# Probabilities transposed by VectorE blocks and DMAs through DRAM for 21 of 24 heads, instead of by TensorE

## The chip, the cores and the metric

The kernel runs on one core of a Trainium2 chip. The metric is the device time of one execution in microseconds; three runs of the kernel before gave 2160.7, 2161.55 and 2162.31 us.

The core's engines work side by side, each through its own instruction stream in order, and wait for one another through semaphores: TensorE (matrix products; PE in the profile, its weight loads PEld), VectorE (DVE), ScalarE (ACT), GpSimd (POOL), and SyncE (SP), which here only issues DMAs. ScalarE and GpSimd can issue DMAs too; the profile shows such issues as ACTq and POOLq.

## The reference

Two decoder layers on 256 tokens of width 2048, all in float32. Layer 0 mixes tokens by attention with a forget gate (FoX, 16 heads of width 128), layer 1 by a mixture of three dilated windows (8 heads, three groups each, values of width 256). Each mixer and each MLP is preceded by a root-mean-square norm. What is around the change is the attention:

```python
def one_block(args):                      # FoX, one block of 128 queries
    i, q_i, c_i = args
    s = jnp.einsum('bqhd,bkhd->bhqk', q_i, k, preferred_element_type=jnp.float32) * scale
    s = s + jnp.transpose(c_i, (0, 2, 1))[..., None] - c_keys[:, :, None, :]
    s = jnp.where(causal, s, -jnp.inf)
    p = jax.nn.softmax(s, axis=-1)
    return jnp.einsum('bhqk,bkhd->bqhd', p.astype(v.dtype), v)
...
s = jnp.where(valid[None, None, :, None], s + alibi, -jnp.inf)     # dilated, one group
m = jnp.max(s, axis=-1)
p = jnp.exp(s - m[..., None])
...
num = jnp.sum(w[..., None] * jnp.stack(nums, 0), axis=0)           # three groups merged
o = (num / den[..., None]).reshape(B, S, H * dv).astype(h.dtype)
```

The product of probabilities and values sums over keys. TensorE sums over partitions, so it needs the probabilities with keys on partitions, while the scores come with queries on partitions: each head's probabilities have to be transposed, three blocks of 128x128 (queries 0 to 127 see one block of keys, queries 128 to 255 see two).

## The kernel before

**Products.** All large products are split so that a float32 factor becomes a high part in the faster fp32r format and a low part that is the rest; a product is then three matmuls (high x high, high x low, low x high). Weights are streamed: SyncE loads `raw` tiles of two 128-row chunks x 512 columns (line 287), ScalarE casts them to `wh` (line 308, the *cast*), VectorE subtracts to get `wl` (line 309, the *cut*). There are five buffers of each. `product_steps` consumes them: one *step* is one 128-row chunk, six matmuls (lines 339 to 341, two token blocks), and after every second step `split` issues the cast and the cut for the buffer pair that has just come free.

**Order of the side work.** The attention chains are Python generators in `Jobs`. After every step `jobs.tick()` resumes those that are due: `yield 4` means "four steps later", `yield key` means "when that key is done". So the order in which work stands in each engine's stream is written out by hand in steps of the product loop. `behind(x)` makes the instructions in its block follow instruction x on the same engine (`issued["cast"]`, `issued["cut"]` and `issued["product"]` are the latest of each).

**FoX.** j runs over four groups of four heads; each j has a query, a key and a value product of 16 steps. `qk_chain` normalizes queries and keys and already transposes them by VectorE's 32x32 blocks, four DMA writes to DRAM per token block (line 543, issued by SyncE) and one read back (line 544, by GpSimd). Then `fox_head` starts for each head hh at step `4 * hh + 2` (for j = 3 at `3 * hh + 2`) after the keys are done: scores on TensorE (lines 714 and 620 to 623), bias, mask and maximum on VectorE (722, 725), exponential on ScalarE (728), normalization on VectorE (733), then `p_transposed`, and three steps later `pv`.

**Dilated heads.** q4 runs over four groups of two heads; `dil_head` starts at step `6 * i + 2`, does scores of the three groups one step apart into the single tile `sd` (line 769), merges the groups into `p` (783 to 786), then `p_transposed`, and two steps later `pv`, twice (two halves of the value's width).

**`p_transposed`** (line 591 on) makes three TensorE transposes into a PSUM bank of the tag `tp` (line 594), then three copies out of it: `p_hi` by ScalarE (598), `p_lo` by VectorE (599), `p_whole` by ScalarE (600). The first two blocks of columns (keys 0 to 127 for both query blocks) are split in high and low; the third stays float32. **`pv`** multiplies them with the values (lines 586 and 587) and copies the result out (588, 589). Work tiles of the tag `s` (scores, probabilities, small constants) share four buffers.

The output projections follow: `out_proj` with `pair=True` runs 12 of 16 chunks for each of the first two column blocks (24 steps), then the last four chunks of each, so that the heads that come last are needed last.

## Time and profile before

| what | value |
|---|---|
| median of three runs | 2161.55 us (2160.7 to 2162.31) |
| the profiled execution's own time | 2161.91 us |
| its span, first to last instruction | 2160.2 us |
| transposes of line 594, FoX heads | 48, in 16 triples |
| transposes of line 594, dilated heads | 24, in 8 triples |
| ScalarE's `p_hi` / `p_whole` copies (lines 598, 600), FoX | 372 ns / 264 ns |
| VectorE's `p_lo` subtraction (line 599) | 417 ns |
| VectorE's block transpose of 128x512 (line 436) | 691 ns |
| bytes moved by all DMAs | 459.34 MB |

In the profile a line such as "182.05 0.49 PE L594 MATMUL ptp_f<-ident,s_f 128*128 128x128 f32 x3" says: at 182.05 us from the start of the span, for 0.49 us, TensorE executed three matmuls of source line 594 that wrote the tile `ptp_f`. Matmuls overlap one another, so what one costs is the distance to the next start, not its own duration. "[1.54 <-PE acc L341]" behind a line is the time for which the engine was idle before it, and what it waited for. A DMA row gives its issuing queue, the size of one, and the median time from issue to landing.

### The profile page before, as it was taken

To read this page: it belongs to the slowest core of one execution; us is meant where nothing else is said; L and a number is where in the kernel's file an instruction comes from. 1 tells how busy PE (TensorE), PEld (TensorE's weight loads), DVE (VectorE), ACT (ScalarE), POOL (GpSimd) and SP (SyncE) were. 2 spreads that over 40 slices of the span, in tenths; PEclk is the share of its full clock that TensorE was granted. 3 is DMA by queue.
4 is the path that set the end of the run, shared out by engine and by line. 5 is a ranking of instruction groups with operands and counts; after the bars stand their busy time and mean duration, and the time that the engine had idled before them with its cause. 6 is when DMAs were issued, how large, how long until landed. Compare 5 with 4: busy or idle time off the path is not lost.

```text
span 2160.2 us, 30057 instructions
## 1 busy us (share of the span) xinstructions
PE 2147.8 (99%) x11208; PEld 1912.6 (89%) x11208; DVE 1397.9 (65%) x1862; ACT 1105.9 (51%) x1545; POOL 74.1 (3%) x92
## 2 busy tenths in 40 slices
PE   9999999999999999999999999999999999999999
PEld 7888888988998998998888888888988988988988
DVE  6777787765655565566668777676655655655664
ACT  6565655644544454455555565546544543544442
POOL 1111000000000000000011010100000000000000
PEclk9999999999999999999999999999999999999999
DMA  7676667766666666667776776758666666666664
GB/s 251 220 225 196 224 201 233 248 203 204 199 203 205 200 201 204 203 199 241 244 242 207 232 226 195 259 177 275 215 204 201 200 204 204 198 203 204 202 210 144
DMA packets 292354, 459.34 MB, mean 213 GB/s; under 512 B 21944, under 2 KB 104432, under 8 KB 292208
## 3 DMA queue, kind: packets, MB, share of 16 engines
q1 hardware_dynamic: 288416, 446.27, 66.1%
q0 software_dynamic: 3232, 10.50, 1.4%
q8 instruction: 87, 1.43, 0.3%
q10 hardware_dynamic: 560, 0.66, 0.1%
q14 instruction: 59, 0.48, 0.1%
HBM read 438.48 MB, written 18.87 MB: 212 GB/s over the span
## 4 chain that ended last, share of the span: by engine, by line
PE 92%; DVE 3%; DMA 2%; issue 1%; ACT 1%; POOL 0%; SPq 0%; DVEq 0%; ACTq 0%; POOLq 0%
PE acc L340 19%; PE acc L341 19%; PE acc L339 19%; PE up_n1a_acc L403 5%; PE up_n3a_acc L403 5%; PE up_n3a_sc L403 3%; PE up_n1a_tp L403 3%; PE up_n1a_sc L403 3%; PE up_n3a_tp L403 3%; PE up_n3a_acc L407 3%; PE up_n1a_acc L407 3%; DMA raw<-in_dil_w_in_dram 2%; DVE wl L309 1%; PE up_n3a_tp L407 1%; PE up_n1a_sc L407 1%; PE up_n1a_tp L407 1%
## 5 line engine op out<-in xcount | busy, mean ns | idle before, releaser
L309 DVE TENSOR_TENSOR wl<-raw,wh 128x1024 fp32r<-128x1024 f32 (+1 forms) x801 | 975.0, 1221 | 686.7 <-ACT wh L308 681.0
L308 ACT CAST wh<-raw 128x1024 fp32r<-128x1024 f32 (+1 forms) x801 | 837.7, 1048 | 931.7 <-PE acc L341 567.4
L339 PE MATMUL acc<-wh,hT_n 128*128 128x512 f32 x896 | 343.0, 384 | 0.5 <-ACT wh L308 0.5
L340 PE MATMUL acc<-wl,hT_n 128*128 128x512 f32 x896 | 339.9, 379 | 0.1
L341 PE MATMUL acc<-wh,hT_n 128*128 128x512 f32 x896 | 339.5, 379 | 0.0
L339 PE MATMUL acc<-wh,aTh_n1a 128*128 128x512 f32 x512 | 194.0, 379 | 0.0
L340 PE MATMUL acc<-wl,aTh_n1a 128*128 128x512 f32 x512 | 194.0, 379 | 0.0
L341 PE MATMUL acc<-wh,aTl_n1a 128*128 128x512 f32 x512 | 194.0, 379 | 0.0
L341 PEld LDWEIGHTS acc<-wh,hT_n 128*128 128x128 f32 x896 | 169.3, 189 | 24.1
L339 PEld LDWEIGHTS acc<-wh,hT_n 128*128 128x128 f32 x896 | 169.6, 189 | 23.4 <-ACT wh L308 0.9
L340 PEld LDWEIGHTS acc<-wl,hT_n 128*128 128x128 f32 x896 | 169.8, 190 | 22.6 <-DVE wl L309 0.4
L339 PE MATMUL acc<-wh,aTh_n3a 128*128 128x512 f32 x480 | 181.9, 379 | 0.0
L340 PE MATMUL acc<-wl,aTh_n3a 128*128 128x512 f32 x480 | 181.9, 379 | 0.0
L341 PE MATMUL acc<-wh,aTl_n3a 128*128 128x512 f32 x480 | 181.9, 379 | 0.0
L403 PE MATMUL up_n1a_acc<-hT_n,wh 128*128 128x512 f32 x512 | 181.6, 382 | 0.0
L403 PE MATMUL up_n3a_acc<-hT_n,wh 128*128 128x512 f32 x512 | 181.6, 382 | 0.0
L407 PE MATMUL up_n1a_acc<-hT_n,wl 128*128 128x256 f32 x512 | 139.6, 273 | 0.0
L407 PE MATMUL up_n3a_acc<-hT_n,wl 128*128 128x256 f32 x512 | 139.6, 273 | 0.0
L341 PEld LDWEIGHTS acc<-wh,aTl_n1a 128*128 128x128 f32 x512 | 96.8, 189 | 13.8
L340 PEld LDWEIGHTS acc<-wl,aTh_n1a 128*128 128x128 f32 x512 | 96.8, 189 | 13.7
L339 PEld LDWEIGHTS acc<-wh,aTh_n1a 128*128 128x128 f32 x512 | 96.8, 189 | 13.6
L403 PEld LDWEIGHTS up_n3a_acc<-hT_n,wh 128*128 128x128 f32 x512 | 96.8, 189 | 13.5
(725 smaller groups left out, 3202.3 us busy)
## 6 DMA issues: line engine op xcount, KB each, us to landing
raw<-in_mlp_w_up_dram SPq DMA_DIRECT2D x256, 512.0 KB, 4.1
raw<-in_mlp_w_down_dram SPq DMA_DIRECT2D x256, 512.0 KB, 4.2
raw<-in_dil_w_in_dram SPq DMA_DIRECT2D x192, 256.0 KB, 4.6
raw<-in_fox_w_in_dram SPq DMA_DIRECT2D x95, 512.0 KB, 4.1
raw<-in_fox_w_out_dram SPq DMA_DIRECT2D x32, 512.0 KB, 4.3
raw<-in_dil_w_in_dram SPq DMA_DIRECT2D x32, 512.0 KB, 4.4
raw<-in_dil_w_out_dram SPq DMA_DIRECT2D x32, 512.0 KB, 4.4
blocks_n<-turned_n SPq DMA_DIRECT2D x96, 64.0 KB, 2.4
```

Of the source, the lines that this page charges most:

```text
L308: issued["cast"] = nc.scalar.copy(hi[:, part, :], raw[:, part, :])
L309: issued["cut"] = nc.vector.tensor_sub(lo[:, part, :], raw[:, part, :], hi[:, part, :].bitcast(F32))
L339: nc.tensor.matmul(acc[t], ah[:, tok], hi, start=first, stop=False)
L340: nc.tensor.matmul(acc[t], ah[:, tok], lo, start=False, stop=False)
L341: issued["product"] = nc.tensor.matmul(acc[t], al[:, tok], hi, start=False, stop=last)
L403: issued["product"] = nc.tensor.matmul(banks[b], hi[:, i, col], in_turn(tokens.rearrange("p x s -> p (x s)"), P // 2), start=first, stop=last)
L407: nc.tensor.matmul(banks[b][:, 0:S], lo[:, i, col], in_turn(tokens[:, 0, :], P // 2), start=False, stop=False)
```

## The change

For all heads but the last two of FoX's j = 3 and the last dilated one, `p_transposed` gives way to two new functions. `p_turned` has VectorE transpose the probabilities in 32x32 blocks into a tile `turned` (tag `s`), writes it to DRAM by four DMAs one step later, and four steps after that reads it back by one DMA, in the order that makes it a full transpose; all five are issued on ScalarE's queue, behind the latest cast. Another four steps later `p_split` makes `p_hi` (ScalarE) and `p_lo` (VectorE, behind the latest cut) from it; the third block is used where it lies. `pv` follows two steps after the split. The split parts are now kept in the order of the tokens, `pv` reads them with the two token blocks interleaved and writes its PSUM tile so; `by_token` undoes this when the result is copied out. `pv`'s matmuls are put behind the latest product. The tag `s` has five buffers instead of four and also holds `p_whole`. The heads of j = 3 start at steps 0, 2, 4, 7 instead of 0, 3, 6, 9, and the second head of q4 = 3 starts 3 steps after the first instead of 6.

```diff
+S_BUFS = 5
...
+    def by_token(po):
+        return po[:, 0:S].rearrange("p (n b) -> p b n", b=2)
...
     def pv(pt_sb, vt, cols, o_hi, o_lo, name):
...
-            for v, p, first in ((v_hi, p_hi, True), (v_hi, p_lo, False), (v_lo, p_hi, False)):
-                nc.tensor.matmul(po[:, 0:S], v[:, c:c + P], in_turn(p, P), start=first, stop=False)
-            nc.tensor.matmul(po[:, P:S], whole[:, c:c + P], p_whole, start=False, stop=True)
-            nc.scalar.copy(o_hi[i], po[:, 0:S])
-            nc.vector.tensor_sub(o_lo[i], po[:, 0:S], o_hi[i].bitcast(F32))
+            with behind(issued["product"]):
+                for v, p, first in ((v_hi, p_hi, True), (v_hi, p_lo, False), (v_lo, p_hi, False)):
+                    nc.tensor.matmul(po[:, 0:S], v[:, c:c + P], p.rearrange("p (b n) -> p n b", b=2), start=first, stop=False)
+                nc.tensor.matmul(by_token(po)[:, 1], whole[:, c:c + P], p_whole, start=False, stop=True)
+            hi, lo = (o.rearrange("p (b n) -> p b n", b=2) for o in (o_hi[i], o_lo[i]))
+            nc.scalar.copy(hi, by_token(po))
+            nc.vector.tensor_sub(lo, by_token(po), hi.bitcast(F32))
+
+    def p_turned(p, name):
+        turned = work.tile([P, 4, 3, 32], F32, tag="s", name=f"turned_{name}", bufs=S_BUFS)
+        nc.vector.transpose(turned.rearrange("p j b r -> p b j r"), p.rearrange("p (b j c) -> p b j c", b=3, c=32))
+        yield 1
+        blocks = dram.tile([4, 32, 4, 3 * 32], F32, tag="pblocks", name=f"pblocks_{name}", bufs=4)
+        for i in range(4):
+            with behind(issued["cast"]):
+                nc.scalar.dma_start(blocks[:, :, i, :].rearrange("j c x -> c j x"),
+                                    turned[32 * i:32 * i + 32].rearrange("p j b r -> p j (b r)"))
+        yield 4
+        with behind(issued["cast"]):
+            nc.scalar.dma_start(turned.rearrange("p i b r -> p (i b r)"), blocks.rearrange("j c i x -> (j c) (i x)"))
+        yield 4
+        return turned
+
+    def p_split(turned, name):
+        p_hi, p_lo = (work.tile([P, S], F32R, tag=f"pT{x}", name=f"pT{x}_{name}", bufs=2) for x in "hl")
+        first = turned.rearrange("p i b r -> p b i r")[:, 0:2]
+        hi, lo = (x.rearrange("p (b i r) -> p b i r", b=2, i=4) for x in (p_hi, p_lo))
+        with behind(issued["cast"]):
+            nc.scalar.copy(hi, first)
+        with behind(issued["cut"]):
+            nc.vector.tensor_sub(lo, first, hi.bitcast(F32))
+        return p_hi, p_lo, turned[:, :, 2, :]
...
     def p_transposed(p, name):
...
-        p_whole = work.tile([P, P], F32, tag="pTw", name=f"pTw_{name}", bufs=2)
-        first = by_column(pt[:, 0:S], P)
-        nc.scalar.copy(halves(p_hi, P), first)
-        nc.vector.tensor_sub(halves(p_lo, P), first, halves(p_hi, P).bitcast(F32))
+        p_whole = work.tile([P, P], F32, tag="s", name=f"pTw_{name}", bufs=S_BUFS)
+        nc.scalar.copy(p_hi, pt[:, 0:S])
+        nc.vector.tensor_sub(p_lo, pt[:, 0:S], p_hi.bitcast(F32))
...
     def fox_head(j, hh, qT, kT, vt, sel):
...
-        yield (3 if j == 3 else 4) * hh + 2
+        yield ((0, 2, 4, 7) if j == 3 else (0, 4, 8, 12))[hh] + 2
...
-        yield 2
-        pt_sb = p_transposed(block(s), f"f{h}")
-        yield ("fv", j)
-        yield 3
+        if j == 3 and hh > 1:
+            yield 2
+            pt_sb = p_transposed(s, f"f{h}")
+            yield 1
+        else:
+            turned = yield from p_turned(s, f"f{h}")
+            yield ("fv", j)
+            pt_sb = p_split(turned, f"f{h}")
+        yield 2
...
     def dil_head(q4, i, qTs, kTs, vt):
...
-        yield 6 * i + 2
+        yield (3 if q4 == 3 else 6) * i + 2
...
-        yield 2
-        pt_sb = p_transposed(block(p), f"d{h}")
-        yield ("dv", q4)
+        if (q4, i) == (3, 1):
+            yield 2
+            pt_sb = p_transposed(p, f"d{h}")
+        else:
+            turned = yield from p_turned(p, f"d{h}")
+            yield ("dv", q4)
+            pt_sb = p_split(turned, f"d{h}")
         yield 2
```

## The prediction

> **What bounds the kernel now.** I read the page first: its busy shares, the chain that ended last, then the waits, the windows and the timelines of single heads.
>
> ```profile
> span 2160.2 us, 30057 instructions
> PE 2147.8 (99%) x11208; PEld 1912.6 (89%) x11208; DVE 1397.9 (65%) x1862; ACT 1105.9 (51%) x1545; POOL 74.1 (3%) x92
> ...
> PE 92%; DVE 3%; DMA 2%; issue 1%; ACT 1%; POOL 0%; SPq 0%; DVEq 0%; ACTq 0%; POOLq 0%
> ```
>
> TensorE leaves 12.4 us idle in 2160.2, and 92% of the ending chain is its own work. So time taken from TensorE is time gained, if nothing that it then waits for is later than before. VectorE and ScalarE have room on average, but not everywhere: the windows show the fox heads of j=1, those of j=3, and the dilated heads of q4=2.
>
> ```profile
> 154.00:190.00 36.00, 36.00 (x194) 32.09 (x193) 29.00 (x60) 22.13 (x47) 1.66 (x1) 1.00 0.61 173
> 292.00:325.00 33.00, 33.00 (x181) 29.65 (x180) 29.34 (x68) 19.19 (x42) 0.53 (x2) 1.00 0.51 168
> 1310.00:1345.00 35.00, 35.00 (x191) 31.32 (x190) 28.58 (x49) 21.16 (x37) 1.66 (x1) 1.00 0.59 189
> ```
>
> Columns after the stretch are PE, PEld, DVE, ACT, POOL busy, granted clock, DMA share. VectorE is busy 81%, 89% and 82% there, ScalarE 61%, 58% and 60%.
>
> **What is removed from TensorE.** The timeline around one head's transposes:
>
> ```profile
> 181.83 0.38 PE L341 MATMUL acc<-wh,hT_n 128*128 128x512 f32 x1
> 182.05 0.49 PE L594 MATMUL ptp_f<-ident,s_f 128*128 128x128 f32 x3
> 182.29 0.46 PE L339 MATMUL acc<-wh,hT_n 128*128 128x512 f32 x1
> 182.59 0.38 PE L340 MATMUL acc<-wl,hT_n 128*128 128x512 f32 x1
> 182.81 0.38 PE L341 MATMUL acc<-wh,hT_n 128*128 128x512 f32 x1
> ```
>
> Matmuls overlap, so I count from start to start. Undisturbed products start every 0.216 us (181.83 to 182.05). The three transposes take 0.24 (182.05 to 182.29), and the product after them takes 0.30 instead of 0.216: together 0.324 us per head. 21 heads: **-6.8 us**. Before the transposes of the first head of q4 = 0, 1 and 3 TensorE also waits, for VectorE's p_d: the first of these is 1.01 us of idle, and all three show 0.70 us for the triple where others show 0.49 (0.21 each). With these transposes gone that is **-1.6 us** (bounds: 0 if the next matmul takes the wait over, -3.3 by the full wait that the line's answer lists).
>
> **What is added on ScalarE's queue.** Per head: four writes of 48 KB, in pieces of 96 x 4 = 384 bytes, and one read of 192 KB, and two copies out of PSUM become one out of SBUF. The nearest rows are the two DMAs that ScalarE's queue issues at the start, and the existing transposes through DRAM on SyncE's queue:
>
> ```profile
> 0.81 0.42 ACTq L916 DMA_DIRECT2D x<-in_x_dram  x1
> ...
> 1.33 0.38 ACTq L291 DMA_DIRECT2D raw<-in_fox_w_in_dram  x1
> ```
> ```profile
> blocks_n<-turned_n SPq DMA_DIRECT2D x96, 64.0 KB, 2.4
> turned_n<-blocks_n SPq DMA_DIRECT2D x24, 256.0 KB, 2.9
> ```
>
> Five issues at 0.40 are 2.0 us per head. Against that, ScalarE loses the p_whole copy (0.27). Four heads in the first window: 22.1 + 4 x 1.73 = 29.1 of 36 us, 81% taken instead of 61%. What also goes is ScalarE's idle wait for VectorE's subtraction before that copy (the waits put it at 15.5 + 10.8 us over 21 waits, 1.25 each), which makes room. On the path: nothing, as long as the weight casts that queue behind the DMAs are at most late by what the five weight buffers cover. A step is six products, 6 x 0.216 = 1.295 us; five buffers of two steps are 13 us, of which cast and cut use 2.3. Without that cover each microsecond of lag would be one of TensorE's.
>
> Will the waits block the queue? The writes are issued from one step after VectorE's transpose, the read four steps (5.2 us) after them, the split four after that. Writes: 4 x 0.40 + 2.4 = 4.0 us, inside 5.2; read 0.4 + 2.9 = 3.3, inside 5.2. I take 0. The DMA rows are 61% loaded or less in these windows and gain 8 MB on 459, so I expect no slower weights. SyncE's and POOL's queues are moved past but get nothing.
>
> The Trainium skill, "DMA: Bandwidth & Descriptors", section Specifications, speaks against these writes: below 512 bytes a piece the DMA engines do a read-modify-write. No run here shows such pieces yet: those of the `blocks` row have 128 x 4 = 512. By that rule the writes land late, which is the slower rival below.
>
> **What is added on VectorE.** One block transpose of 128x384: by the row of 128x512 (691 ns) 0.52 us. The subtraction reads SBUF, like the 128x256 of line 562 (about 0.49), instead of PSUM (0.417): +0.07. So +0.6 us per head, 2.4 us in a window of 36: 81% becomes 87%, 89% (two heads in 33 us) becomes 93%. Not a bound by itself, but it sets when p_lo is ready. Reading po by a stride of two costs nothing: line 598 reads PSUM that way in 0.372, line 588 contiguously in 0.365. The last p.v matmul now writes PSUM with a stride of two; no row shows that. Bounds: 0, and doubled, 0.14 us x 32 pairs = 4.5 us. I take 0, since all its other numbers (128 columns, fp32, two passes) stay.
>
> **The shorter wait ahead of p.v.** For fox heads p.v followed three steps after the transposes; now two steps after the split (the dilated ones stay at two). The split falls on a step that also casts weights, as it already did for the dilated heads. So an old dilated head shows the race (ScalarE, VectorE, TensorE; TensorE's step ended at 1425.66):
>
> ```profile
> 1425.86 1.05 ACT L308 CAST wh<-raw 128x1024 fp32r<-128x1024 f32 x1 [1.54 <-PE acc L341]
> 1426.81 0.37 ACT L598 CAST pTh_d<-ptp_d 128x256 fp32r<-128x256 f32 x1
> ```
> ```profile
> 1426.94 1.22 DVE L309 TENSOR_TENSOR wl<-raw,wh 128x1024 fp32r<-128x1024 f32 x1 [0.96 <-ACT wh L308]
> 1428.08 0.42 DVE L599 TENSOR_TENSOR pTl_d<-ptp_d,pTh_d 128x256 fp32r<-128x256 f32 x1
> ```
>
> p_lo is done 2.84 us after the step's end; with the 0.07 above 2.91. Two steps later, without transposes between, TensorE wants it at 2 x 1.295 + 0.11 = 2.70. Late by 0.21, with the semaphore some 0.25 us. Head 0 of each j is covered by head 3's scores between (0.73 us), j=3's two heads by other heads' work. That leaves 9 heads: **+2.3 us** (bounds: 0; 14 x 0.45 = 6.3, where 0.45 comes from the latest such subtraction, 3.44 us after its step at 315.35, less the transposes). For dilated heads the count of steps moves the split from a casting step to the one between, where fox subtractions ended 1.4 to 1.7 us after the step: 0.
>
> **Starts that move.** j=3's heads start at 0, 2, 4, 7 instead of 0, 3, 6, 9 steps. The last p.v then lies at step 17; the pair's steps for chunks 12 to 15 begin after 24: 7 steps of cover, 9 us. For q4=3 head 7 starts after 3 steps, not 6, while head 6 still uses the only `sd` tile until its step 7: its third scores can wait for a PSUM bank. The nearest row is a score's wait for VectorE's sd (1.3 us in two, longest 0.7): **+0.7** (bounds 0 and 3, about the adds, one weight cut and one score pass on VectorE). The fifth `s` buffer keeps writers from waiting: at most five such tiles live at once.
>
> **Sum.** -6.8 - 1.6 + 2.3 + 0.7 = -5.4 us. The profiled execution took 2161.91 (span 2160.2 and 1.7 around it), 0.36 above the median 2161.55. I forecast 2161.55 - 5.4 = **2156.2 us**; alone it ranges from 2152.5 (late p_lo and bank waits 0, p_d waits a little larger) to 2160.
>
> **Rivals.** A: late operands ahead of p.v give it back. For: VectorE at 87 to 93%, and the query chain of the next j keeps it busy without a gap from 183 to 190 us, just where heads 2 and 3 are to be split. Against: 24 waits of this kind cost TensorE almost nothing before. At the upper bound +6.3 in place of +2.3: 2160.2; with doubled strided writes too, 2164.7. I set it at 2161.
> B, the slower one: ScalarE's queue blocks at the read, since the writes land late. If they land at 4.8 us, twice the 2.4 of the row (single rows of such writes show up to 3.7), 1.6 + 4.8 = 6.4 against 5.2: each read holds the queue 1.2 us. A fox round of four steps and a head's work (6.5 us) then has on ScalarE two casts 2.1, both copies 0.7, exponentials 1.0, issues 2.0, wait 1.2: 7.0, more than the round, and the query chain's squares (1.4) on top; p_hi slips by 0.5 us a round, and by 0.35 more with the squares spread over four heads. At 0.85 us for 18 heads (the first of j = 0, 1, 2 is covered) that is +15.3; with -8.4 from TensorE, 2161.55 - 8.4 + 15.3 = 2168.5. It decides from a landing above some 3.6 us (5.2 - 1.6), and is slower by 0.2% from 0.7 us a head on. Against: four steps are wider than the landing rows. The Trainium skill's rule named above would make it this one.
>
> **How the numbers follow.** Forecast 0.55, A 0.20, B 0.25. About 0.2% (4.3 us: below 2157.2 or above 2165.9) is what a measurement of this kernel can tell from no change. Of the forecast 0.42 lies below 2157.2 and 0.13 within; A is within for 0.17 and slower for 0.03; B is slower for 0.23 and within for 0.02. Faster 0.42, same 0.32, slower 0.26. The range goes from 2152.5 to 2169, leaving out the worse half of B and a few hundredths below 2152.5.
>
> **What would show it.** Right: 9 transposes left (three heads), ACTq rows of 0.4 us, TensorE's idle still near 12 us, p.v's second matmul 0.1 to 0.4 us after the first. Wrong: long waits of p.v for ScalarE (B: with ScalarE's DMA waiting for `pblocks`), of products for wh or wl (the cover gone), or a longer last matmul of p.v.

## The result, and the profile after

The changed kernel takes 2164.99 us in the median of 22 runs (2162.74 to 2169.07), the kernel before beside it 2161.57 us: a ratio of 1.0019, interval 1.0013 to 1.0025. It is slower, by 2.8 to 5.4 us. 2156.2 had been forecast.

The page of the changed kernel (its profiled run took 2163.54 us), first the span and the engines' busy time, then the chain that ended last:

```profile
span 2161.8 us, 30098 instructions
PE 2145.2 (99%) x11145; PEld 1908.7 (88%) x11145; DVE 1407.9 (65%) x1883; ACT 1098.2 (51%) x1524; POOL 75.7 (4%) x92
...
PE 92%; DVE 3%; DMA 2%; ACT 1%; issue 1%; POOL 0%; SPq 0%; DVEq 0%; ACTq 0%; POOLq 0%
```

63 matmuls are gone (11145 for 11208), but TensorE's busy time falls by 2.6 us only, and its idle time rises from 12.4 to 16.6. The shares of the chain say nothing: they are the same as before. Where TensorE stood shows in the waits of the changed kernel (engine, tile and line, what it waited for, then us in all, times, longest):

```profile
PE sc_f L660 <- ACT fkT_0h L561: 5.6, 4, 2.5
...
PE po_d L593 <- DVE pTl_d L625: 1.4, 2, 0.7
...
PE sc_d L657 <- DVE sd L806: 1.1, 2, 0.8
```

The same view of the kernel before has one wait of the first kind:

```profile
PE sc_f L623 <- ACT fkT_0h L560: 1.1, 1, 1.1
```

So the scores of the first FoX head of each group j wait for ScalarE's copy of the keys' high part (line 560 before, 561 after). The change touches neither the step at which these heads start nor the code of that copy. The timeline of TensorE in the changed kernel at group 1:

```profile
153.44 0.33 PE L746 MATMUL sc_f<-negc,sel 128*128 128x384 f32 x1
153.61 0.38 PE L657 MATMUL sc_f<-fkT_0w,fqT_0w 128*128 128x128 f32 x2
155.83 0.38 PE L660 MATMUL sc_f<-fkT_0h,fqT_0h 128*128 128x256 f32 x1 [1.84 <-ACT fkT_0h L561]
...
157.13 0.54 PE L341 MATMUL acc<-wl,hT_n 128*128 128x512 f32 x1
157.47 0.63 PE L342 MATMUL acc<-wh,hT_n 128*128 128x512 f32 x1
157.90 0.63 PE L340 MATMUL acc<-wh,hT_n 128*128 128x512 f32 x1
```

The gap is 1.84 us, and a second loss follows it: products that take 0.38 us and start every 0.216 take 0.63 and start every 0.43. The windows of one microsecond show why (after PE, PEld, DVE, ACT, POOL busy comes the granted clock):

```profile
156.00:157.00 1.00, 1.00 (x7) 0.91 (x8) 0.74 (x3) 1.00 (x2) 0.00 (x0) 1.00 0.91 236
157.00:158.00 1.00, 1.00 (x5) 0.79 (x4) 1.00 (x2) 0.05 (x1) 0.00 (x0) 0.61 0.89 315
158.00:159.00 1.00, 1.00 (x4) 0.81 (x3) 1.00 (x4) 0.86 (x1) 0.00 (x0) 0.50 0.17 66
159.00:160.00 1.00, 1.00 (x3) 0.75 (x3) 1.00 (x2) 1.00 (x5) 0.00 (x0) 0.50 0.52 63
160.00:161.00 1.00, 1.00 (x5) 0.82 (x4) 0.96 (x4) 0.07 (x1) 0.00 (x0) 0.68 0.81 283
```

From 157.13 to 160.76 TensorE starts nine products in 3.63 us, where 9 x 0.216 = 1.94 would do: 1.7 us lost. The gaps of groups 0 to 3 are 0.33, 1.84, 0.97 and 2.50 us; the half clock follows the second and the fourth.

By stage, from the first and last starts of tiles on TensorE in one profile each (us; "6" is experiment 6 below, "9" experiment 9):

| | before | after | 6 | 9 |
|---|---|---|---|---|
| first score of FoX | 85.3 | 85.2 | 87.2 | 85.0 |
| first product of the first MLP | 379.1 | 383.0 | 374.9 | 380.9 |
| first dilated score | 1152.8 | 1156.7 | 1148.6 | 1154.6 |
| first product of the second MLP | 1490.0 | 1491.6 | 1483.8 | 1492.5 |
| last product | 2156.4 | 2158.1 | 2150.3 | 2159.0 |

FoX loses 3.9 us; that stage repeats well (379.0 to 379.2 in three kernels with FoX's transposes on TensorE, 374.6 to 375.2 in three like 6). The dilated stage takes 334.9 us for 337.2, but single profiles of it spread: 334.8 to 338.0, mean 336.1, over the eleven kernels here with its 7 heads by DMA and TensorE's 21 transposes gone; 335.5 to 337.2, mean 336.4, over the six without. So most of the 2.3 us (7 x 0.324) that TensorE is spared there comes back as waits. The rest does not move.

**Why the keys are late.** The key chain goes from VectorE's block transposes of the normalized keys over SyncE's writes, GpSimd's read and ScalarE's copies to the scores. From the timelines, counted from the start of the first of these transposes in groups 1, 2 and 3: the end of the `fkT_0h` copy ("ready"), and the start of the score that needs it, less its wait ("needed").

| us after the transposes | ready | needed | to spare |
|---|---|---|---|
| before | 16.35, 16.12, 16.34 | 16.66, 16.66, 16.90 | 0.31, 0.54, 0.56 |
| after | 17.40, 16.53, 18.05 | 15.61, 15.61, 15.60 | -1.79, -0.92, -2.45 |
| 6 | 17.40, 14.84, 16.30 | 16.91, 16.66, 17.06 | -0.49, 1.82, 0.76 |
| 9 | 17.22, 16.57, 18.06 | 17.28, 17.09, 17.34 | 0.06, 0.52, -0.72 |
| 14 | 17.79, 17.41, 18.03 | 15.61, 15.61, 15.60 | -2.18, -1.80, -2.43 |

Before, the keys were ready 0.3 to 0.6 us ahead. After, TensorE is at the score 1.05 to 1.3 us sooner after the transposes, and the keys are ready 0.4 to 1.7 us later. "Sooner" does not mean that TensorE gets faster from the keys' product to their scores. To see that, count from the end of the key product, which is where ScalarE starts to square it (the changed kernel's row, then the one before, group 1):

```profile
127.89 0.69 ACT L519 ACTIVATE sq_('fk', 1)_0_1432<-acc,rstd_n 128x512 f32<-128x512 f32 x1 [0.69 <-PE acc L342]
```
```profile
130.64 0.69 ACT L518 ACTIVATE sq_('fk', 1)_0_1424<-acc,rstd_n 128x512 f32<-128x512 f32 x1
```

| us after the first square, groups 1, 2, 3 | transposes start | ready | needed |
|---|---|---|---|
| before | 8.64, 8.64, 8.40 | 24.99, 24.75, 24.75 | 25.29, 25.29, 25.29 |
| after | 10.49, 10.49, 10.49 | 27.89, 27.02, 28.54 | 26.10, 26.10, 26.10 |
| 9 | 8.76, 8.76, 8.76 | 25.99, 25.33, 26.81 | 26.04, 25.85, 26.10 |

Counted so, TensorE comes to the score 0.8 us later than before: between product and score stand 115 product matmuls as before, and now also one head's p.v of the group before. What got longer is the chain, by 1.85 to 2.1 us ahead of the transposes (the first half) and by 0.4 to 1.7 us behind them (the second half).

The first half: TensorE ends group 1's key product 2.7 us sooner than before, since four heads' transposes (1.3 us) are gone, the wait at group 0 is 0.8 us shorter and the p.v just named has moved behind. But VectorE's transposes come only 0.9 us sooner. VectorE in the changed kernel, then in the kernel before:

```profile
132.51 0.36 DVE L530 TENSOR_SCALAR rq_('fk', 1)_1440<-rq_('fk', 1)_1440,rstd_n 128x4 f32<-128x4 f32 x2 [1.78 <-POOL rq_('fk', 1)_1440 L526]
...
135.98 0.42 DVE L563 TENSOR_TENSOR fqT_0l<-sq_('fq', 1)_0_1207,fqT_0h 128x256 fp32r<-128x256 f32 x1
136.32 0.42 DVE L563 TENSOR_TENSOR fqT_1l<-sq_('fq', 1)_0_1207,fqT_1h 128x256 fp32r<-128x256 f32 x1
...
137.25 1.22 DVE L310 TENSOR_TENSOR wl<-raw,wh 128x1024 fp32r<-128x1024 f32 x1
138.38 0.71 DVE L540 STREAM_TRANSPOSE sq_('fk', 1)_0_1432<-qn_('fk', 1)_0_1475 128x512 f32<-128x512 f32 x1
```
```profile
138.68 0.68 DVE L531 TENSOR_TENSOR qn_('fk', 1)_1_1470<-acc,rq_('fk', 1)_1432 128x512 f32<-128x512 f32 x1
139.28 0.70 DVE L539 STREAM_TRANSPOSE sq_('fk', 1)_0_1424<-qn_('fk', 1)_0_1467 128x512 f32<-128x512 f32 x1
```

After, VectorE works without a break from 132.51 on, and has the query chain's cuts and one more weight cut ahead of the keys. The second half is on SyncE's queue, the changed kernel first:

```profile
134.03 2.43 SPq L288 DMA_DIRECT2D raw<-in_fox_w_in_dram  x2
139.12 1.77 SPq L544 DMA_DIRECT2D blocks_('fk', 1)_0_1481<-sq_('fk', 1)_0_1432  x4
140.99 1.85 SPq L544 DMA_DIRECT2D blocks_('fk', 1)_1_1488<-sq_('fk', 1)_1_1434  x4
142.94 15.84 SPq L288 DMA_DIRECT2D raw<-in_fox_w_in_dram  x9
```
```profile
138.79 0.37 SPq L287 DMA_DIRECT2D raw<-in_fox_w_in_dram  x1
140.01 1.77 SPq L543 DMA_DIRECT2D blocks_('fk', 1)_0_1473<-sq_('fk', 1)_0_1424  x4
141.88 1.83 SPq L543 DMA_DIRECT2D blocks_('fk', 1)_1_1480<-sq_('fk', 1)_1_1426  x4
143.81 14.82 SPq L287 DMA_DIRECT2D raw<-in_fox_w_in_dram  x8
```

SyncE now reaches the key writes one weight load sooner and stands from 136.46 to 139.12 until VectorE has transposed. No load goes out for 6.5 us (136.46 to 142.94) instead of 4.7 (139.16 to 143.81). ScalarE's cast waits for the load, and the key copies stand behind the cast:

```profile
141.99 1.05 ACT L309 CAST wh<-raw 128x1024 fp32r<-128x1024 f32 x1 [1.54 <-PE acc L342]
147.85 1.04 ACT L309 CAST wh<-raw 128x1024 fp32r<-128x1024 f32 x1 [4.80 <-DMA raw<-in_fox_w_in_dram]
149.87 1.05 ACT L309 CAST wh<-raw 128x1024 fp32r<-128x1024 f32 x1 [0.98 <-DMA raw<-in_fox_w_in_dram]
150.82 0.51 ACT L554 ACTIVATE fkT_0w<-qn_('fk', 1)_0_1475,gain 128x256 f32<-128x256 f32 x1
```

In groups 2 and 3 the casts wait 4.75 and 6.23 us in the same place; before, no cast waits there for a load. Which of the two halves is the lever was not clear from the traces alone. That is what most of the experiments are about.

### The profile page after: what moved, and what is told of

The parts are those of the page before. It is cut to its first block, busy times and chain, and to the rows that moved or that the text cites. A ratio compares the mean times of both kernels' runs of the same rounds, so it can differ in the third digit from the quotient of the medians.

```text
span 2161.8 us, 30098 instructions
## 1 busy us (share of the span) xinstructions
PE 2145.2 (99%) x11145; PEld 1908.7 (88%) x11145; DVE 1407.9 (65%) x1883; ACT 1098.2 (51%) x1524; POOL 75.7 (4%) x92
## 4 chain that ended last, share of the span: by engine, by line
PE 92%; DVE 3%; DMA 2%; ACT 1%; issue 1%; POOL 0%; SPq 0%; DVEq 0%; ACTq 0%; POOLq 0%
PE acc L341 19%; PE acc L340 19%; PE acc L342 19%; PE up_n1a_acc L404 5%; PE up_n3a_acc L404 5%; PE up_n1a_sc L404 3%; PE up_n1a_tp L404 3%; PE up_n3a_tp L404 3%; PE up_n3a_sc L404 3%; PE up_n3a_acc L408 3%; PE up_n1a_acc L408 3%; PE up_n3a_sc L408 1%; PE up_n3a_tp L408 1%; PE up_n1a_tp L408 1%; PE up_n1a_sc L408 1%; DVE wl L310 1%
```

## The experiments

Each was timed beside the kernel before on the same chip; ratios are to that. Experiments 1 to 4 ran first.

**1. The key writes one step later**, so that SyncE's order has eight loads ahead of them again.

```diff
     def qk_chain(acc, tag, key, parts):
...
+        later = 1 if key[0] == "fk" and key[1] else 0
+        if later:
+            yield later
         for t in range(NT):
             turned = sq[t].rearrange("p (j h r) -> p j h r", j=4, h=4)
...
-        yield 10
+        yield 10 - later
```

> The key chain's block transposes and its DMA writes on SyncE's queue come one step later for j = 1 to 3 (the step is taken back from the wait behind them), which lets the eighth weight load go ahead of them again, as in the kernel before. Theory (a weight load stuck behind the key chain's writes on SyncE's queue makes a cast late, the cast makes the keys late, and TensorE waits and then runs at half clock): line 660's waits for fkT_0h at j = 1, 2, 3 fall from 1.8, 1.0 and 2.5 us to under 0.3, the granted clock is 1.00 around 157 to 160 and 297 to 300 us, and the time is 2165.0 - 5 - 3.4 = 2156.5, give or take 1.5. Rival (the loss lies in the new path of the probabilities itself): the waits go but the time stays above 2162.

Measured: 2164.15 us, ratio 1.0013 (1.0004 to 1.0022). The order has eight loads again, but the writes start at 141.67 and loads resume only at 145.49; casts still wait 3.23, 2.66 and 4.70 us, and the gaps of groups 0 to 3 are 1.47, 1.02, 0.28 and 2.26. The count of loads alone cures nothing if the writes move too. The runs sort by granted clock: 2160.2 to 2162.4 at 1.000 (four), 2162.8 to 2164.2 at 0.999 (three), 2164.7 to 2168.7 at 0.998 (four): the time of one and the same kernel rises as its clock falls. (Longer waits may come with a lower clock; the one run of it with a profile has no half clock.)

**2. Work for TensorE in the gap**: fourteen transposes of the identity between the first head's two score blocks.

```diff
-        for t in range(NT):
-            scores(ps, t, qT[hh // 2], kT[hh // 2], hh % 2, True)
+        scores(ps, 0, qT[hh // 2], kT[hh // 2], hh % 2, True)
+        if j and not hh:
+            fill = ps_tp.tile([P, P], F32, tag="tp", name=f"fill{j}")
+            for _ in range(14):
+                nc.tensor.transpose(fill, ident, ident)
+        scores(ps, 1, qT[hh // 2], kT[hh // 2], hh % 2, True)
```

> 14 transposes of the identity, into a bank that nothing reads, stand on TensorE between the scores of query block 0 and 1 of the first head of j = 1, 2, 3, where it waits for the keys (1.1 us of work by start-to-start distances of 0.08). Theory (the wait is what brings the clock down): granted clock 1.00 throughout, the waits shorter by what the fillers take, the time some 3 us below the changed kernel, 2162. Rival (the clock falls for another reason): it is 0.5 for 3.4 us as before, and the time is within 1 us of 2165.

Measured: 2163.65 us, 1.0011 (1.0003 to 1.002); the clock is 1.000 in all 11 runs, where 21 of 22 runs of the changed kernel lie at 0.997 to 0.999. The keys are as late as ever, so the gap is what brings the half clock. The fillers use up most of what that saves.

**3. The change without its DMAs**: new layout, strided p.v and starts, but all 24 heads transposed on TensorE.

```diff
-        if j == 3 and hh > 1:
+        if True:
...
+            yield ("fv", j)
...
-        if (q4, i) == (3, 1):
+        if True:
...
+            yield ("dv", q4)
```

> All 24 heads are transposed by TensorE, with the new layout of p, the strided PSUM write, the five buffers and the new starts kept. Theory: these cost nothing, 2161.5 give or take 1. Rival (the strided write of p.v doubles its last matmul): 2166, and line 594's pairs at 0.28 us from start to start instead of 0.14.

Measured: 2161.7 us, 1.0003 (0.9994 to 1.0012). Layout, the strided PSUM write and the new starts cost nothing that can be seen (by the interval at most 2.6 us; doubled strided writes would have cost 4.5).

**4. The FoX heads alone** by DMA, the dilated ones on TensorE.

```diff
-        if (q4, i) == (3, 1):
+        if True:
...
+            yield ("dv", q4)
```

> Only the 14 fox heads go through VectorE and DMAs, the dilated ones through TensorE. Theory: the whole loss is here, 14 x 0.324 = 4.5 us gained against 5.3 of waits and 3.4 of clock: 2165 to 2167, with line 660's waits for fkT_0h as in the changed kernel. Rival (the dilated part loses): 2161 or less.

Measured: 2168.14 us, 1.0032 (1.0021 to 1.0042), gaps of 1.15, 1.96, 0.97 and 3.24 us, clock 0.998. The loss is in the FoX part.

**5. FoX's query and key writes on GpSimd**, so that SyncE issues loads only.

```diff
-                nc.sync.dma_start(blocks[:, :, i, :].rearrange("j c x -> c j x"),
+                (nc.gpsimd if tag == "n0" else nc.sync).dma_start(blocks[:, :, i, :].rearrange("j c x -> c j x"),
...
```

> The changed kernel, with the block writes of the fox heads' query and key chains issued by GpSimd instead of SyncE, so that SyncE never stands still for VectorE's transposes between two weight loads. Theory (the new waits of TensorE for fkT come from SyncE's queue: a weight load stands behind key writes that wait for VectorE, ScalarE's cast waits for that load, and the key copies queue behind the cast): ScalarE's waits for raw loads of the gate weights fall from 16 us to under 8, the waits of scores for fkT to near 1 us in all, the granted clock stands at 1.00 and the time is 2157.5 us, 2156 to 2160. Rival (the key copies are late since ScalarE issues the probabilities' DMAs and waits at their reads): the waits of scores for fkT stay above 4 us, clock 0.998, 2163 to 2165.

Measured: 2188.69 us, 1.0129 (1.0115 to 1.0143). Neither theory had this. GpSimd's queue at group 1:

```profile
148.76 2.22 POOL L544 DMA_DIRECT2D blocks_('fk', 1)_0_1481<-sq_('fk', 1)_0_1432  x4 [1.02 <-DVE sq_('fk', 1)_0_1432 L540]
150.97 1.64 POOL L544 DMA_DIRECT2D blocks_('fk', 1)_1_1488<-sq_('fk', 1)_1_1434  x3
156.27 0.57 POOL L545 DMA_DIRECT2D qn_('fk', 1)_0_1475<-blocks_('fk', 1)_0_1481  x1 [3.66 <-issue]
156.83 0.56 POOL L544 DMA_DIRECT2D blocks_('fk', 1)_1_1488<-sq_('fk', 1)_1_1434  x1
```

The read of the first half stands ahead of the last write of the second and waits for data, 3.66 us. Keys come so late that gaps of 2 to 4 us open twice in each of groups 1 to 3.

**6. All FoX heads one step (six products, 1.3 us) later.**

```diff
-        yield ((0, 2, 4, 7) if j == 3 else (0, 4, 8, 12))[hh] + 2
+        yield ((0, 2, 4, 7) if j == 3 else (0, 4, 8, 12))[hh] + 3
```

> The changed kernel with the scores of all fox heads one step of the order (about 1.3 us of products) later; nothing else moves. Theory (keys late by 1 to 2.5 us, and each gap above some 1.2 us costs another 1.7 us by the clock): the gaps shrink by 1.3 us each, to about 0.5 and 1.2 us, the clock returns to 1.00, the time is 2159.5 us, 2158 to 2162. Rival (what delays the keys moves along with the heads, since the key copies wait for buffers that the heads free): waits for fkT stay at 5 to 6 us, 2163 to 2166.

Measured: 2156.26 us (2155.01 to 2158.19), ratio 0.9979 (0.997 to 0.9988), clock 1.000 in all ten runs: faster than both kernels, and than the 2158 to 2162 expected. Its page and its waits:

```profile
span 2154.0 us, 30095 instructions
PE 2142.2 (99%) x11145; PEld 1906.9 (89%) x11145; DVE 1408.4 (65%) x1883; ACT 1098.0 (51%) x1524; POOL 73.0 (3%) x92
```
```profile
PE po_d L593 <- DVE pTl_d L625: 1.5, 2, 0.7
PE sc_d L657 <- DVE sd L806: 1.3, 2, 1.0
PE sc_f L660 <- ACT fkT_0h L561: 0.5, 1, 0.5
```

Of the key waits 0.5 us is left, and FoX ends at 374.9 instead of 379.1 (before). At group 1 a cast still waits 4.75 us for a load, and the keys are ready 17.40 us after the transposes as in the changed kernel; only TensorE comes later. In groups 2 and 3 the chain itself is faster too.

**7. The dilated heads alone** by DMA, FoX on TensorE.

```diff
-        if j == 3 and hh > 1:
+        if True:
...
+            yield ("fv", j)
```

> The change for the 7 dilated heads alone: the 17 fox heads transpose their probabilities on TensorE as in the kernel before. Theory (all of the loss lies in the fox part): the 21 transposes of the dilated heads, 2.3 us, come off TensorE's time and no wait for fkT above 1.2 us appears; clock 1.00, 2159.0 us, 2157.5 to 2160.5. Rival (the write and read on ScalarE's queue give back what the transposes save, in the dilated part too): 2161 to 2164.

Measured: 2162.52 us, 1.0008 (0.9999 to 1.0017), clock 1.00. The 2159 expected did not come: the dilated stage takes 336.8 us, 0.4 less than before instead of 2.3. In that stage casts wait 12.8 us for loads (before 3.3), and TensorE's scores wait 2.5 us in three for `sd` (before 1.3 in two). By 4 beside the changed kernel (ratios 1.0032 and 1.0019) the dilated heads seemed worth 2.8 us; here they lose 1.8 (interval -0.2 to 3.7). What they are worth by themselves stays open.

**8. A control: the kernel before, heads earlier.**

```diff
-        yield (3 if j == 3 else 4) * hh + 2
+        yield (3 if j == 3 else 4) * hh or 1
```

> A control: the kernel before, with no DMA for probabilities at all, but with the scores of the first fox head one step and of the other fox heads two steps of the order earlier. Theory (a late key by itself costs the wait and, where the wait is above some 1.2 us, a stretch at half clock of some 1.7 us): waits for fkT at the first head of each group grow by about 1.3 us to 5 us in all, the granted clock in the steps behind them falls to 0.5 and the time rises to 2166 us, 2164 to 2172. Rival (the half clock comes from something in the changed kernel, its DMAs or its missing transposes): the gaps grow, the clock stays at 1.00 and the time is 2162 to 2166 by the gaps alone.

Measured: 2164.02 us, 1.0014 (1.0005 to 1.0023), clock 1.00; gaps 1.96, 0.72, 0.45, 0.45. They did not grow by the 1.3 us expected: the score now comes 24.24 us after the first square instead of 25.29, which is 1.05 us sooner, and the 0.31 to 0.56 us that the keys had to spare come off that. The one long gap brought no half clock.

**9. The transposes back as idle work**, all DMAs kept.

```diff
         yield 4
+        spent = ps_tp.tile([P, 3 * P], F32, tag="tp", name=f"spent_{name}")
+        for b in range(3):
+            nc.tensor.transpose(spent[:, b * P:(b + 1) * P], ident, ident)
         return turned
```

> The changed kernel with all its DMAs, and in addition three transposes of the identity on TensorE for each of the 21 heads, into a PSUM tile that nobody reads, behind the read of the turned probabilities: TensorE's work is as long as before, all else is as in the changed kernel. Theory (the keys' chain has a fixed length; TensorE reaches the scores earlier by 4 x 0.324 = 1.3 us in each group of four fox heads, since the transposes between a group's key products and its scores are gone, and that eats a slack of some 0.7 us): with the transposes back the gaps at the groups' first heads shrink from 1.84, 0.97 and 2.50 us to under 1 us each, the granted clock is 1.00 and the time 2162 us, 2160.5 to 2164. Rival (the DMAs alone make the keys late: SyncE stands still before the key writes, weight loads and casts behind it are late): the gaps stay at 1.5 to 2.5 us with half clock behind them, 2167 to 2172.

Measured: 2165.14 us, 1.0019 (1.0011 to 1.0028), above the range; clock 1.00. In groups 1 and 2 the gaps are gone, in group 3 0.77 us is left, in group 0 1.40. The DMAs by themselves therefore do not open the long gaps. The table that counts from the first square shows what changed. All twelve idle transposes of a group lie ahead of the next key product's end, so TensorE ends that product later; from there VectorE's transposes come after 8.76 us instead of 10.49, while the score is needed at 25.9 to 26.1 as in the changed kernel. So the first half of the lateness goes away when TensorE is held back ahead of the product, with all of the change's work still on VectorE. The second half stays: the keys are ready 17.2, 16.6 and 18.1 us after the transposes, as in the changed kernel. It belongs to the rest of the change, and its cause was not found. That the kernel is still 4 us above the one before was not followed further; `sd` (2.1 us) and `pTl_d` (1.6) are also waited for. At group 1 no cast waits for a load any more:

```profile
146.79 1.05 ACT L309 CAST wh<-raw 128x1024 fp32r<-128x1024 f32 x1 [1.54 <-PE acc L342]
149.38 1.05 ACT L309 CAST wh<-raw 128x1024 fp32r<-128x1024 f32 x1 [1.54 <-PE acc L342]
151.10 0.51 ACT L554 ACTIVATE fkT_0w<-qn_('fk', 1)_0_1491,gain 128x256 f32<-128x256 f32 x1 [0.67 <-DMA qn_('fk', 1)_0_1491<-blocks_('fk', 1)_0_1497]
```

SyncE's order has eight loads here, so this run does not yet tell VectorE's lateness from the order of the load; 14 does.

**10. A control: the kernel before, heads one step later.**

```diff
-        yield (3 if j == 3 else 4) * hh + 2
+        yield (3 if j == 3 else 4) * hh + 3
```

> A control: the kernel before, with the scores of all fox heads one step of the order later, the same edit that made the changed kernel 2156.3 us. Theory (the edit only takes waits for the keys away, and before has but one, 1.15 us at the first group): that wait shrinks and the time is 2160.3 us, 2159 to 2161.5. Rival (a later start is worth some 4 us by itself, whoever transposes the probabilities): 2156 to 2158.

Measured: 2164.64 us, 1.0016 (1.0007 to 1.0025). The key wait shrinks to 0.33 us, but p.v then waits 1.09 us three times for `pTl_f`, and the time rises by 3.5. The later start is no gain by itself; it pays only where the keys are what is late.

**11. Experiment 6 with the dilated p.v a step later.**

```diff
             pt_sb = p_split(turned, f"d{h}")
+            yield 1
         yield 2
```

> The changed kernel with the fox heads one step later, and p.v of the dilated heads one step further behind the split of the turned probabilities. Theory (p.v's weight loads wait 2.5 us for pTl_d and 0.8 us for pTh_d, since VectorE and ScalarE come to the split late; one step of 1.3 us covers that): those waits fall under 0.5 us in all and the time is 2154.0 us, 2152.5 to 2155.5. Rival (what is waited for moves along, as a tile of p that is freed later holds the next head back): 2156 to 2158.

Measured: 2156.82 us, 0.9981 (0.9972 to 0.9989): nothing gained on 6. The waits for `pTl_d` stay at 1.4 us.

**12. FoX's query and key writes on ScalarE**, behind the latest cast.

```diff
-                nc.sync.dma_start(blocks[:, :, i, :].rearrange("j c x -> c j x"),
+                with behind(issued["cast"]):
+                    (nc.scalar if tag == "n0" else nc.sync).dma_start(blocks[:, :, i, :].rearrange("j c x -> c j x"),
...
```

> The changed kernel with the block writes of the fox heads' query and key chains issued by ScalarE, each behind the last weight cast, instead of by SyncE; SyncE issues weight loads alone there. Theory (the cast's wait of 4.8 us for a load behind the key writes on SyncE is a half of what makes the keys late): ScalarE's waits for raw loads of the gate's weights fall from 16 us to under 8, the gaps at the groups' first heads to under 1 us, clock 1.00, 2158.5 us, 2157 to 2161. Rival (eight more issues of 0.45 us and the wait for VectorE's blocks now hold ScalarE, and the casts and key copies with it): gaps of 2 us and more, 2165 to 2175.

Measured: 2183.08 us, 1.01 (1.0084 to 1.0115); the rival, and worse than its numbers. ScalarE's queue at group 1:

```profile
145.21 1.77 ACTq L545 DMA_DIRECT2D blocks_('fk', 1)_0_1481<-sq_('fk', 1)_0_1432  x4
147.08 2.13 ACTq L545 DMA_DIRECT2D blocks_('fk', 1)_1_1488<-sq_('fk', 1)_1_1434  x4
149.25 3.96 ACT L309 CAST wh<-raw 128x1024 fp32r<-128x1024 f32 x4 [7.09 <-PE acc L342]
```

No cast is made for 7.09 us while the queue waits for VectorE and issues; the gaps are 4.2 to 4.3 us.

**13. A control: the kernel before, key writes a step later and heads two steps earlier.** The edit of 1, and:

```diff
-        yield (3 if j == 3 else 4) * hh + 2
+        yield (3 if j == 3 else 4) * hh
```

> A control: the kernel before, with the block writes of the key chains of groups 1 to 3 one step of the order later and the scores of all fox heads two steps earlier; no DMA for probabilities, all transposes on TensorE. e8 had gaps of 0.72, 0.45 and 0.45 us at groups 1 to 3 with the first heads one step earlier; one step more and later writes add 1.3 us each. Theory (a gap of TensorE above some 2 us brings the half clock, whatever made the gap): gaps of 2.5 to 3.3 us at groups 1 to 3, 0.50 of the clock for some 3 us behind each, clock 0.997, time 2172 us, 2168 to 2177. Rival (the half clock needs something of the changed kernel, its DMAs or its missing transposes): gaps as long, clock 1.00, 2166 to 2168.

Measured: 2165.02 us, 1.0015 (1.0006 to 1.0024), gaps 2.29, 0.93, 0.45, 0.45, clock 1.00. The long gaps wanted at groups 1 to 3 did not come, since neither edit moved what it was meant to: the transposes start 8.64, 8.64 and 8.40 us after the first square, as before, and the score whose keys are late stands at 24.25 us, where it stood in 8, because six products now lie between a head's two score blocks. Whether a gap of 2.5 us in the kernel before brings the half clock was not reached.

**14. The load ahead of the key writes by order alone.**

```diff
+            ahead = key[0] == "fk" and key[1]
+            while ahead and state["raw"] < state["split"] + 5:
+                load()
             for i in range(4):
+              with behind(*([issued["load"]] if ahead else [])):
                 nc.sync.dma_start(blocks[:, :, i, :].rearrange("j c x -> c j x"),
...
```

> The changed kernel; only the fifth weight load ahead is written down before the block writes of the key chains of groups 1 to 3, and these are issued behind it, so that SyncE's order has 8 loads between a group's query writes and its key writes, as the kernel before has, where the changed kernel has 7 (2 becomes 3 in group 3). VectorE's transposes and ScalarE's copies stay at their steps. Theory (the load that slipped behind the key writes is what makes a cast wait 4.8, 4.75 and 6.2 us, the key copies queue behind that cast, TensorE's gaps and the half clock follow): no cast of groups 1 to 3 waits over 2 us for a load, the gaps fall under 0.6 us, clock 1.00, time 2157.5 us, 2156 to 2160. Rival (the keys are late since TensorE reaches the scores 1.3 us earlier, whatever the loads do): gaps of 1 to 2.5 us stay, 2161.5 to 2165.

Measured: 2164.62 us, 1.0018 (1.0009 to 1.0027), gaps 0.33, 2.23, 1.85, 2.48. The theory fell. ScalarE at group 1:

```profile
148.56 1.04 ACT L309 CAST wh<-raw 128x1024 fp32r<-128x1024 f32 x1 [2.36 <-DMA raw<-in_fox_w_in_dram]
151.75 0.51 ACT L558 ACTIVATE fkT_0w<-qn_('fk', 1)_0_1475,gain 128x256 f32<-128x256 f32 x1 [2.14 <-DMA qn_('fk', 1)_0_1475<-blocks_('fk', 1)_0_1481]
```

The cast's wait is halved, from 4.80 to 2.36 us, and the copy now waits 2.14 us for its own data instead: the writes go out behind the load. On one queue, what the load gains the keys lose.

**15. Two loads ahead:** the edit of 14 with `+ 6` for `+ 5`.

> As e14 with a sixth load ahead: 9 loads between a group's query and key writes. The sixth needs a buffer that a cast frees only later, so SyncE holds the key writes back for it. Theory: no long wait of a cast for a load, but the key writes start some 2.6 us later and the keys with them; gaps of 1 to 2.5 us, 2161 to 2165. Rival (more loads ahead are simply better): gaps under 0.6 us and no more than e14's time.

Measured: 2179.76 us, 1.0082 (1.0069 to 1.0096): the direction of the theory, at several times its size, with gaps of 3.74 us or more in groups 1 to 3 and shorter ones ahead of them.

**16. Experiments 6 and 14 together.**

> e14 with the fox heads' scores one step later as in e6. Theory (e6 has one gap of 0.54 us left at group 1, behind a cast that waited 4.75 us for a load; both edits cure the same thing): at most 1 us less than e6, 2155.5 us, 2154 to 2157. Rival (the late start costs what it cost in the kernel before, 3.5 us, as soon as the keys are in time): 2158 to 2161.

Measured: 2156.5 us, 0.9979 (0.9971 to 0.9988), the same as 6. With the later start the order of the load is worth nothing.

## Why the prediction was wrong

**The step that failed** is "time taken from TensorE is time gained, if nothing that it then waits for is later than before", with the check that followed it: "On the path: nothing, as long as the weight casts that queue behind the DMAs are at most late by what the five weight buffers cover" and "SyncE's and POOL's queues are moved past but get nothing". The prediction looked for lateness in what the change touches, p.v and the casts; of VectorE's added work it says "Not a bound by itself, but it sets when p_lo is ready". It did not look at the next group's keys, whose chain runs over the same VectorE, SyncE and ScalarE. The keys had 0.31 to 0.56 us to spare in the profile of before, readable there. After the change TensorE reaches the end of the key product sooner (2.7 us in group 1), VectorE does not follow, and counted from that end the keys are ready 2.3 to 3.8 us later, while TensorE wants them only 0.8 us later. TensorE waits 5.3 us for them in groups 1 to 3. Putting the time back on TensorE (9) or giving the keys one step (6) removes all but 0.8 and 0.5 us of these waits; moving the load (14) or the writes (1, 5, 12) does not. That the chain cannot keep up with a faster TensorE is thus shown. Which of VectorE's instructions ahead of the transposes starts it is read from the trace and was not tried by itself, and why the chain behind the transposes takes 0.4 to 1.7 us longer stays open.

**The number.** 2165 lies inside the range, just above A at its worst (2164.7) and below B (2168.5). That is chance: neither A's late operands ahead of p.v nor B's blocked queue made it, as the terms below show.

**The size.** From the changed kernel to 6 FoX ends 8.1 us sooner: 5.1 from the waits (0.33 + 1.84 + 0.97 + 2.50 less 0.54) and 3.4 from two half clocks of 1.7; the 0.4 too much is what single profiles differ by. The half clock stood in no case of the prediction.

**-6.8 for the transposes**: about right for FoX, which with its keys in time ends 4.2 us sooner (14 x 0.324 is 4.5), though 0.6 us of that is a shorter wait for keys (0.54 us in 6, 1.15 before). Of the dilated heads' 2.3 hardly anything is left on average (the stage's means above).

**-1.6 for the waits for `p_d`**: they are gone, but p.v of the dilated heads now waits 1.4 us for `pTl_d` in their place (0.72 us each in the groups q4 = 1 and 2). The prediction had put that lateness at 0 for these heads.

**+2.3 for `p_lo` of nine FoX heads**: 0. No `po_f` stands among the waits; the step's products lie between p.v's first and second matmul (107.8 and 109.2 us at the first head), which the prediction had assumed to be neighbours.

**+0.7 for the second head of the last dilated group**: 0.3 in the trace of the changed kernel, where before has no such wait; 0.8 in 4 and 9. The waits for `sd` are 1.1 us in two: 0.78 in the first dilated group (before 0.65) and 0.30 here.

**0 for the strided PSUM write**: nothing seen (3).

**"I expect no slower weights"**: not so in FoX. Its weights land 4.8 us after the issue in the median, before 4.1, and the casts wait 16.3 us in all for them, before 5.7. The median is 4.4 to 5.0 us in all twelve profiles with FoX heads by DMA and 3.9 to 4.3 in the six without. Whether this is the second half of the keys' lateness was not tried.

**ScalarE's queue, rival B**: an issue costs 0.34 to 0.44 us, as taken. The rows of the changed kernel (KB of one, us to landing):

```profile
pblocks_f<-turned_f ACTq DMA_DIRECT2D x56, 48.0 KB, 3.2
...
pblocks_d<-turned_d ACTq DMA_DIRECT2D x28, 48.0 KB, 2.8
```

The writes of 384-byte pieces land in 2.8 to 3.2 us, under the 3.6 from which B decides. The Trainium skill's rule on pieces under 512 bytes ("DMA: Bandwidth & Descriptors", Specifications) may show in that, since the 512-byte writes of `blocks_n` land in 2.1, but it does not double the time, and no run separates the size of the pieces from the stage and the queue. ScalarE waits for its own writes four times, 13.9 us in all, where 0 was taken; no wait of TensorE is traced to it.

**The sum** of -5.4 was that of a kernel whose keys are in time: 6, with one number changed, is at -4.5 us (-6.5 to -2.6) against the kernel before. That it comes so near is in part luck: the +2.3 that is 0 partly makes up for the -1.6 and the dilated heads' -2.3, which brought next to nothing.

## What to carry to other kernels

Before work is taken off the engine that bounds a kernel, list every chain that this engine meets again later (here the next group's keys) and read from the profile how long its result lay ready: an engine that gets faster by more than that can wait for what the edit never touched. Count from the end of the faster engine's own product: a chain that runs over busy engines (here VectorE) need not move with it. Such slack is cheap to give back by starting the consumer a step later, which is worth a try before anything else; moving the key writes to another engine's queue cost 18 and 24 us against the changed kernel, since the late writes held up what stood behind them there (the rows of 5 and 12). A wait of two microseconds on TensorE can cost nearly twice its length (1.84 us and 1.7 behind it).

## What the runs showed of the hardware

A long gap of TensorE brings a stretch at half clock, but not always. Gaps of 1.84 and 2.50 us (changed kernel), 1.96 (4), 1.85 and 2.48 (14) did; gaps of 1.96 (8), 2.29 (13), 2.26 (1 and 15) and 2.23 (14) did not. The records of the granted clock in the 18 traces say what tells them apart. From some 10 us on, where they begin:

- Every slow stretch among the products lasts 3.41 us or two or three times that (5 and 15). In each profile all of them, with the one that follows the last matmul, start a whole number of 3.4133 us apart: 22, 44, 298 and 591 of them in 12, and 41 and 587 in the changed kernel. So the clock is set in windows of 3.41 us that run through the whole execution, and the stretch behind the last matmul gives their position where there is no other.
- Add up TensorE's idle time, as the profile has it, in each window up to 2150 us that runs at full clock. Where it is 1.80 us or less (1.80 in 13, 1.75 in 5, 1.74 in 8, 1.67 in 14), the next window runs at full clock; where it is 1.84 or more (1.84 in the changed kernel, 1.85 in 14, 1.96 in 4, and all above), the next one runs at half. No window of the 18 profiles is an exception.

A gap that falls across two windows can therefore be longer and bring nothing: the 2.26 us of 1 are 1.49 and 0.77, those of 15 are 1.24 and 1.02, and the 2.23 of 14 are 0.56 and 1.67. This would also explain why one kernel falls in it or not from run to run (1), if its windows lie otherwise each time. The rule was read from the profiles afterwards; no run was made to test it.

The Trainium skill ("TensorE: Matmul & The Clock Gate", HAM oscillation) warns of idle gaps above about 3.4 us, and its Part 1 says that the activity window of that length runs freely. The windows here agree with the second; the limit does not agree, since 1.84 us in one window was enough.
